# Input projection by seven block products, with K, Q, V, gate and x through DRAM, and attention after all projections

## The chip, the cores and the metric

One core of a Trainium2 chip runs the whole kernel. The metric is device time in microseconds. TensorE is called PE (its weight loads PEld), VectorE DVE, ScalarE ACT, GpSimd POOL, and SyncE SP; SP only issues transfers here.

## The reference

One decoder layer on 1024 tokens of width 1024, all in float32: a norm, one input projection, two kinds of heads side by side, an output projection, and a gated FFN.

```python
n = rmsnorm(h, mix_norm_w)
proj = n @ w_in                       # 1024 x 5648: [z 1024 | x 1024, B 256, C 256 | dt 16 | q 1024 | k 1024 | v 1024]
xbc = silu(causal_dwconv(xbc))        # width 4, along tokens
# SSD heads (16 of 64, 2 groups, state 128), in chunks of 128 tokens
cb = einsum("bclgn,bcsgn->bcgls", cm, bm)
y_diag = einsum("bcgls,bgecls,bcsgep->bclgep", cb, lmat, xdt)
y_off = einsum("bclgn,bcgepn,bgecl->bclgep", cm, prev_states, exp(a_cs))
y = (y_diag + y_off + x5 * d_skip) * silu(z), then a norm in each group, times ssd_norm_w
# differential attention (8 heads, two maps of 64, values of 128), causal, in blocks of 128 queries
p = softmax(where(mask, s, -inf)); w = p[0] - lam * p[1]; o = w @ v, then a norm in each head
h = h + concat(y_ssd, y_da) @ w_out
h = h + (silu(n2 @ w_gate) * (n2 @ w_up)) @ w_down
```

## The kernel before

**Precision.** A float32 factor is split into a high part in a short format (`hi`, a cast on ACT) and the rest (`lo`, a subtraction on DVE, both in `split`), and a product is three matmuls, hi x hi, hi x lo and lo x hi (`mm3`, lines 127 to 129). Transposes, the scan's products and the values' product (`o`) take float32 as it is; the trace shows two passes for each of the latter.

**Order.** The kernel is written as one sequence of tile operations. A scheduler then orders each engine's instructions, and may put later ones ahead where their inputs and buffers allow; only around the output projection's last part and the first FFN pair is PE's order kept as written. Pools of tiles set how far that goes: `big` (4 tiles of 16 KB for each partition, `B16`), `a4` (14 of 4 KB), `p4` (6), `cv` (4), `hx` (3), `raw` (2), `wh` and `wl` (3 each), and in PSUM `mm` (2 banks), `sc` (2 of two banks) and `ms` (2 banks).

**Stages.**
- The rows of x are normed (`norm_rows`), transposed and split (`norm_transpose`): `nhi` and `nlo`, two halves of 512 tokens, fill the four big tiles until the last head's Q.
- `proj_T` makes 128 columns of the projection as [columns, 512 tokens], 24 matmuls of 512 columns for each half of the tokens: for x, B and C (with the convolution), and for K and Q of each head. `proj_nat` makes 256 columns as [128 tokens, 256], for the gate and V; `proj_z0` the first gate columns together with the 16 of dt.
- The scan of a group of SSD heads (`ssd_scan`) runs over 8 chunks, each in three steps (`front`, `middle`, `back`); `back` stores the transposed y to `yT_d`. Its inputs `CT`, `Bn`, `CB` and `xn` stay in SBUF; the gate comes from `z_d` in DRAM.
- Attention runs over 8 heads and, in each, 8 blocks of 128 queries. A pair of heads gets its V by `v_pair`, a head its K and Q by `qk`, whose sinks write `KS`, `QH` and `QL` straight from PSUM. For each block and each of the two maps, PE makes scores `s` in one of the two `sc` buffers, DVE adds the mask and takes the maximum, ACT does the exponential and its sum, DVE combines the maps (line 596), PE transposes the weights (`wtp`), ACT copies them, and PE multiplies by V (`o`, line 611). `att_back` of a block comes after `att_front` of the next.
- The output projection takes `yT_d` back in four groups of 512 rows (`load_y`: weighted by the norm's weights as it is split), adding each group's 256-column products to the sums in DRAM or SBUF: `po_s` for the first group, `po_a` for the next two, `po_b` for the last.
- The FFN's gate and up projections, and then the down projection, are made by seven products of half-size blocks (Winograd's form) instead of eight: sums of weight blocks on POOL (`sub`), sums of the normed rows' blocks once ahead (`turn` and `room` make their transposed, split operands), and sums of the products by adding on in PSUM and reading between (`ORDER`).

Of the kernel before, what the change touches and what calls it, by code (L numbers as in the profile page):

```python
# [24 lines left out]
def tile_hybrid_block(  # L25
# [86 lines left out]

    def norm_transpose(parts, wbc, his, los, t, xn, pts, name, pool=()):
        norm_rows(parts, wbc, [xn], name, pool)
        tk = slice((t % 4) * P, (t % 4) * P + P)
        for q in range(2):
            pt = pts([P, 4, P], f"pt_{name}_{q}")
            for j in range(4):
                k = q * 4 + j
                nc.tensor.transpose(pt[:, j, :], xn[:, k * P:(k + 1) * P], ident)  # L120
            hi = his[t // 4][:, q * 4:q * 4 + 4, tk]
            lo = los[t // 4][:, q * 4:q * 4 + 4, tk]
            nc.scalar.copy(hi, pt)
            nc.vector.tensor_tensor(lo, pt, hi.bitcast(F32), op=ALU.subtract)
# [45 lines left out]
    def split(hi, lo, raw, scale=None):  # L170
        if scale is None:
            nc.scalar.copy(hi, raw)  # L172
            nc.vector.tensor_tensor(lo, raw, hi.bitcast(F32), op=ALU.subtract)  # L173
# [17 lines left out]
    def z0_unit(raw, a, u):
        hi = wp.tile([P, 4, 264], F32R, tag="wh", bufs=3, name=f"wh_z0_{a}_{u}")
        lo = wp.tile([P, 4, 264], F32R, tag="wl", bufs=3, name=f"wl_z0_{a}_{u}")
        split(hi, lo, raw)
        return hi, lo

# [49 lines left out]


    def proj_T(*jobs):
        """each job: a weight, a column, a name and sink(half, psum [128 columns, 512 tokens])"""
        us = [w_unit(w_k[:, :, col:col + P], [P, KD, P], name) for w_k, col, name, _ in jobs]  # L250
        for half in range(2):
            for (hi, lo), (_, _, name, sink) in zip(us, jobs):
                ps = MM([P, 512], f"mm_{name}_{half}")
                for k in range(KD):
                    mm3(ps, hi[:, k, :], lo[:, k, :], nhi[half][:, k, :], nlo[half][:, k, :], k == 0, k == KD - 1)
                sink(half, ps)

    def proj_z0(us, name, sink):
        """units of 264 columns; sink(t, psum [128 tokens, 264])"""
        for t in range(NT):  # L260
            ps = (MS if t % 4 > 1 else MM)([P, 264], f"mm_{name}_{t}")
            tk = slice((t % 4) * P, (t % 4) * P + P)
            for k in range(KD):
                hi, lo = us[k // 4]
                mm3(ps, nhi[t // 4][:, k, tk], nlo[t // 4][:, k, tk], hi[:, k % 4, :], lo[:, k % 4, :],
                    k == 0, k == KD - 1)
            sink(t, ps)

    def proj_nat(col, name, sink):
        """256 columns; sink(t, psum [128 tokens, 2 blocks from t, 256])"""  # L270
        us = [w_unit(w_in_k[:, 4 * u:4 * u + 4, col:col + 256], [P, 4, 256], f"{name}_{u}") for u in range(2)]
        for t in range(0, NT, 2):
            ps = MM([P, 2, 256], f"mm_{name}_{t}")
            for i in range(2):
                tk = slice(((t + i) % 4) * P, ((t + i) % 4) * P + P)
                for k in range(KD):
                    hi, lo = us[k // 4]
                    mm3(ps[:, i, :], nhi[t // 4][:, k, tk], nlo[t // 4][:, k, tk], hi[:, k % 4, :], lo[:, k % 4, :],
                        k == 0, k == KD - 1)
# [55 lines left out]
    def conv_tiles(*tiles):  # L335
        jobs = []
        for ct, name, acc in tiles:
            u_ = CV([P, T], F32, "u_" + name)
            jobs.append((ct, name, acc, u_))

        def wk(ct, k):
            return pcol[:, CW + k * 12 + ct:CW + k * 12 + ct + 1]

        def sink_of(ct, name, acc, u_):
            def sink(half, ps):
                sl = slice(half * 512, half * 512 + 512)
                nc.scalar.copy(u_[:, sl], ps)
                nc.scalar.activation(acc[:, sl], ps, AF.Identity, bias=pcol[:, CB + ct:CB + ct + 1], scale=wk(ct, 3))
            return sink
        proj_T(*[(w_in_k, C_X + j[0] * P, j[1], sink_of(*j)) for j in jobs])  # L350
        for ct, name, acc, u_ in jobs:
            for sh in (1, 2, 3):
                nc.vector.scalar_tensor_tensor(acc[:, sh:], u_[:, :T - sh], wk(ct, 3 - sh), acc[:, sh:],
                                               op0=ALU.mult, op1=ALU.add)
            nc.scalar.activation(acc, acc, AF.Silu)

    def gate_dt():
        """the gate of group 0 and dt"""
        for a in range(2):
            zt = [None]  # L360
            w0, w = (0, 248) if a == 0 else (248, 264)

            def sink(t, ps):
                if t % 2 == 0:
                    zt[0] = CV([P, 2, w], F32, f"zt0_{a}_{t}")
                if a == 0:
                    nc.vector.tensor_tensor(adt[:, t, :], ps[:, 0:16], hv[:, 0, :], op=ALU.add)
                nc.scalar.activation(zt[0][:, t % 2, :], ps[:, 264 - w:], AF.Silu)
                if t % 2 == 1:
                    nc.gpsimd.dma_start(z_d[t - 1:t + 1, :, w0:w0 + w].rearrange("t p c -> p t c"), zt[0])  # L370
            proj_z0(zus if a == 0 else [z0_unit(z0_raw(1, u), 1, u) for u in range(2)], f"z0_{a}", sink)

    def gate(g):
        for hf in range(2):
            zt = [None]
            zc = g * 512 + hf * 256

            def sink(t, ps):
                if t % 4 == 0:
                    zt[0] = CV([P, 4, 256], F32, f"zt{g}_{hf}_{t}")  # L380
                nc.scalar.activation(zt[0][:, t % 4:t % 4 + 2, :], ps, AF.Silu)
                if t % 4 == 2:
                    nc.gpsimd.dma_start(z_d[t - 2:t + 2, :, zc:zc + 256].rearrange("t p c -> p t c"), zt[0])
            proj_nat(C_Z + zc, f"z{g}_{hf}", sink)

    def ssd_inputs(g):
# [27 lines left out]
        for j in range(4):  # L414
            xc = CV([P, T], F32, f"xc{g}_{j}")
            conv_tiles((g * 4 + j, f"x{g}_{j}", xc))
            if prev is not None:
                turn(j - 1, prev)
# [663 lines left out]
```

## Time and profile before

| | |
|---|---|
| Median of three runs | 1643.02 us (1641.4 to 1645.18) |
| Profiled execution: its span, with nothing shown around it | 1643.3 us |
| Busy: PE, DVE, ACT, POOL | 1597.2, 1071.6, 775.8, 429.2 us |
| Projections, scans and attention, by the trace | start to about 840 us |
| Rest of the output projection, then FFN and final norm | 840 to 960, 960 to 1643 us |

How to read it: "PE busy" joins modelled matmul times, so a busy PE streams without a pause, though one matmul's time (0.39 us for 512 columns) overlaps the next's; the pace is the time between two starts. In a row of groups stand the line, the engine, the operation, out<-in by tile names, the shape and the count, then the sum of busy time, the mean of one in ns, and the engine's idle time just ahead of them with who ended it.

### The profile page before, as it was taken

The page shows a single profiled execution, that of the slowest core. Times are in us where ns is not written, and L with a number is a line of the kernel's source. Part 1 is how long each engine was busy: PE and PEld are TensorE (multiplying, and loading weights), DVE is VectorE, ACT ScalarE, POOL GpSimd, SP SyncE. Part 2 cuts the span into 40 slices and gives each one's busy share as a digit, 9 for nine tenths or more (in the row PEclk, how much of TensorE's full clock was granted, in tenths as well). Part 3 has the DMA queues.
Part 4 walks back from the last instruction along what each step waited for, and adds up shares of the span by engine and source line. Part 5 has one row for each costly group of instructions (what it writes and reads, how often), then busy time and mean ns, then how long its engine had stood idle before and what let it go on. Part 6 is the DMA issues. An engine that isn't in the chain of part 4 may idle for free. (4 is left out here: it accounts for less than half of the span.)

```text
span 1643.3 us, 23716 instructions
## 1 busy us (share of the span) xinstructions
PE 1597.2 (97%) x9170; PEld 1386.9 (84%) x9170; DVE 1071.6 (65%) x1682; ACT 775.8 (47%) x1608; POOL 429.2 (26%) x378
## 2 busy tenths in 40 slices
PE   6999999999999999999999998999999999999997
PEld 6988878887989989889999987888888888778885
DVE  5345745688776676677674477455555555898987
ACT  6444764456555565575552245333333333334445
POOL 4100330032000000013300034444444443542322
PEclk9999999999999999999999999999999999999999
DMA  5321451143011110147523221233333323944122
GB/s 195 110 79 52 129 163 56 36 142 92 24 46 39 46 33 27 45 130 229 162 77 116 84 99 56 96 102 104 111 116 118 98 96 134 365 166 186 39 103 103
DMA packets 105291, 172.78 MB, mean 105 GB/s; under 512 B 7813, under 2 KB 75530, under 8 KB 103770
## 3 DMA queue, kind: packets, MB, share of 16 engines
q1 hardware_dynamic: 95210, 137.11, 25.2%
q0 software_dynamic: 9968, 34.15, 6.3%
q8 instruction: 72, 1.18, 0.3%
q14 instruction: 41, 0.34, 0.1%
HBM read 125.82 MB, written 45.42 MB: 104 GB/s over the span
## 5 line engine op out<-in xcount | busy, mean ns | idle before, releaser
L127 PE MATMUL x<-n,wa 128*128 128x512 f32 x352 | 138.7, 396 | 0.0
L128 PE MATMUL x<-n,wa 128*128 128x512 f32 x352 | 138.7, 394 | 0.0
L129 PE MATMUL x<-n,wa 128*128 128x512 f32 x352 | 137.8, 394 | 0.0
L590 ACT ACTIVATE p<-s,nmx 128x256 f32<-128x256 f32 (+7 forms) x128 | 94.4, 740 | 53.2 <-DVE nmx L588 49.9
L172 ACT CAST wa<-s 128x512 fp32r<-128x512 f32 x88 | 54.7, 622 | 132.3 <-PE x L129 59.4
L173 DVE TENSOR_TENSOR wa<-s,wa 128x512 fp32r<-128x512 f32 x88 | 76.8, 873 | 51.1 <-ACT wa L172 50.8
L172 ACT CAST dg<-gd 128x512 fp32r<-128x512 f32 x77 | 47.7, 620 | 114.7 <-PE dx L129 57.2
L588 DVE TENSOR_REDUCE nmx<-s 128x1 f32<-128x256 f32 (+7 forms) x128 | 95.3, 754 | 2.4
L173 DVE TENSOR_TENSOR dg<-gd,dg 128x512 fp32r<-128x512 f32 x77 | 66.2, 862 | 23.3 <-ACT dg L172 23.2
L129 PEld LDWEIGHTS x<-n,wa 128*128 128x128 f32 x352 | 66.5, 189 | 15.1
L128 PEld LDWEIGHTS x<-n,wa 128*128 128x128 f32 x352 | 66.6, 189 | 14.8
L127 PEld LDWEIGHTS x<-n,wa 128*128 128x128 f32 x352 | 66.6, 189 | 14.8
L127 PE MATMUL mm_z<-wh_z,nhi 128*128 128x264 f32 (+1 forms) x256 | 75.9, 298 | 2.3 <-ACT wh_z L172 2.3
L611 PE MATMUL o<-v,p 128*128 128x128 f32 x576 | 77.7, 275 | 0.0
L129 PE MATMUL mm_z<-wh_z,nlo 128*128 128x264 f32 (+1 forms) x256 | 77.3, 303 | 0.0
L611 PEld LDWEIGHTS o<-v,p 128*128 128x128 f32 x576 | 73.5, 191 | 2.7
L128 PE MATMUL mm_z<-wl_z,nhi 128*128 128x264 f32 (+1 forms) x256 | 75.0, 294 | 0.0
L127 PE MATMUL mm_v<-wh_v,nhi 128*128 128x256 f32 x256 | 74.2, 290 | 0.0
L129 PE MATMUL mm_v<-wh_v,nlo 128*128 128x256 f32 x256 | 74.1, 290 | 0.0
L128 PE MATMUL mm_v<-wl_v,nhi 128*128 128x256 f32 x256 | 73.5, 287 | 0.0
L128 PE MATMUL po_a<-wl_wo,yh 128*128 128x256 f32 x256 | 72.6, 283 | 0.0
L91 POOL TENSOR_TENSOR rs_o<-ms_o,mhalf 128x4 f32<-128x4 f32 x16 | 18.0, 1125 | 208.4 <-DVE ms_o L89 208.3
(331 smaller groups left out, 5172.9 us busy)
## 6 DMA issues: line engine op xcount, KB each, us to landing
gd<-g_d SPq DMA_DIRECT2D x11, 1792.0 KB, 7.8
wr_g<-in_w_gate_dram SPq DMA_DIRECT2D x22, 512.0 KB, 3.8
wr_u<-in_w_up_dram SPq DMA_DIRECT2D x22, 512.0 KB, 4.3
g_d<-sg SPq DMA_DIRECT2D x22, 512.0 KB, 5.1
wr_d<-in_w_down_dram SPq DMA_DIRECT2D x22, 512.0 KB, 5.0
L<-cs_d POOLq DMA_DIRECT2D x16, 512.0 KB, 4.4
wr_y<-yT_d SPq DMA_DIRECT2D x16, 512.0 KB, 3.8
wr_wo<-in_w_out_dram SPq DMA_DIRECT2D x16, 512.0 KB, 3.5
```

Of the source, the lines that this page charges most:

```text
L91: nc.gpsimd.tensor_tensor(r, ms, mhalf[:, :w], op=ALU.pow)
L127: nc.tensor.matmul(ps, lh, rh, start=first, stop=False, skip_group_check=more)
L128: nc.tensor.matmul(ps, lh, rl, start=False, stop=False, skip_group_check=more)
L129: nc.tensor.matmul(ps, ll, rh, start=False, stop=last, skip_group_check=more)
L172: nc.scalar.copy(hi, raw)
L173: nc.vector.tensor_tensor(lo, raw, hi.bitcast(F32), op=ALU.subtract)
L588: nc.vector.reduce_max(nmx[:, m:m + 1], s[:, :Lk], axis=AX.X, negate=True)
L590: nc.scalar.activation(p[:, :Lk], s[:, :Lk], AF.Exp, bias=nmx[:, m:m + 1], accum_out=sm[:, m:m + 1])
L611: nc.tensor.matmul(o, wT[:, j * P:(j + 1) * P], vt[h % 2][j], start=(j == 0), stop=(j == i))
```

## The change

The input projection is made by the seven products too. The normed rows' seven operands (`room`, `turn`, now defined ahead) stand in the four big tiles (products 1, 2, 6, 5) and in twelve of the `a4` tiles (7, 3, 4) until the last projection. `in_pair` replaces `proj_T`, `proj_nat` and `proj_z0`: for two column tiles it makes seven products, the sums of weight blocks on POOL, and reads PSUM seven times, copying on ACT or adding on DVE. dt has matmuls of its own (`dt_cols`). What it yields goes to DRAM: `z_d`, `v_d`, `kT_d`, `qT_d`, `xn_d` (x transposed) and `bc_d` (C, B and their product), and is loaded again for each chunk or head; the scan and `qk` read from there.

The order written is: gate of group 0, dt, B, C, x; then the second gate and V with scan 0 woven in between products (`weave`), K and Q of head pairs with scan 1; then attention for all heads. The first two groups of the output projection are one (`po_s` over eight row tiles), `po_a` the third.

Other moves: the norms' weights are applied where y is stored (four ACT products for each chunk instead of a copy; `oT`), so `load_y` splits without a factor, with the subtraction on POOL; the subtractions for `KS` and `QL` are on POOL; the stores of `yT_d` and `h_d`, and the loads of x for the sums, are issued by SP instead of POOL.

```diff
+    def in_pair(a, s5, name, wide, outs, sink, scale=None):
+        sub(s5, a[1][0], a[1][1], ALU.add)
+        sub(a[1][0], a[0][0], a[1][0])
...
+        for p in ORDER:
...
+            src = {1: a[0][0], 2: a[0][1], 6: a[0][0], 5: s5, 7: a[1][0], 3: a[0][1], 4: a[1][1]}[p]
...
+            if wide:
+                for k0 in (0, 2):
+                    at = wp.tile([P, 2, 2, 256], F32R, tag="wh", bufs=3, name=f"wa_{name}_{p}_{k0}")
+                    split(at[:, 0], at[:, 1], src[:, k0:k0 + 2, :])
...
+            else:
+                at = wp.tile([P, 2, 4, P], F32R, tag="wh", bufs=3, name=f"wa_{name}_{p}")
+                split(at[:, 0], at[:, 1], src)
+                for k in range(4):
+                    mm3(ps[0], at[:, 0, k, :], at[:, 1, k, :], bh[k], bl[k], new and k == 0, k == 3, True)
...
-    gate_dt()
+    for _ in wide_pair(C_Z, "z0", sink_z(0), zraw, z0_out, P4([P, 4, 256], F32, "s5_z0")):
+        pass
+    dt_cols()
     decays()
-    ssd_scan(0, *ssd_inputs(0))
-    gate(1)
-    ssd_scan(1, *ssd_inputs(1))
+    for col, name, sk in ((C_B, "B", sink_bc("B")), (C_C, "C", sink_bc("C")), (C_X, "x0", sink_x(0)),
...
+    weave([(lambda: wide_pair(C_Z + 512, "z1", sink_z(1)), 14),
+           (lambda: wide_pair(C_V, "v0", sink_v(0)), 14),
+           (lambda: wide_pair(C_V + 512, "v1", sink_v(1)), 14)], ssd_scan(0), 30 / 42)
...
+           for h in range(0, NH, 2) for c, d, n, sc in ((C_K, kT_d, "k", None), (C_Q, qT_d, "q", 0.125))],
+          ssd_scan(1), 30 / 50)
...
     def qk(h):
...
+            kd, qd = [CV([P, 2, 512], F32, f"{n}d{h}_{half}") for n in "kq"]
+            for t_, src in ((kd, kT_d), (qd, qT_d)):
...
+            nc.scalar.copy(ks, kd)
+            for m in range(2):
+                b = slice(64 - 64 * m, 128 - 64 * m)
+                sub(ks[b, m, :], kd[b, m, :], ks[b, m, :].bitcast(F32))
+            split(qh, ql, qd, nc.gpsimd)
...
-            split(yh[:, j, :], yl[:, j, :], load_raw(yT_d[kt], [P, T], f"y{kt}"), scale=pcol[:, col:col + 1])
+            split(yh[:, j, :], yl[:, j, :], load_raw(yT_d[kt], [P, T], f"y{kt}"), nc.gpsimd)
...
-    ys = [load_y(0)]
+    ys = [load_y(0), load_y(1)]
...
-    for kg in (1, 2):
+    for kg in (2,):
```

Three places in the engines' orders. The first is PE at the first scores of head 0 (`s0_0_0`: head, block, map). Before, they stand among the products for K of head 1 (`mm_k1`), with the scan still going (`ytp1_6`):

```order
L127 MATMUL mm_k1_1_3785<-nhi1_135,wh_k1_3751 128x512
L585 MATMUL s0_0_0_3453<-KS0_0_3340,QH0_0_3406 128x128
L586 MATMUL s0_0_0_3453<-KS0_0_3340,QL0_0_3407 128x128
L128 MATMUL mm_k1_1_3785<-nlo1_137,wh_k1_3751 128x512
L129 MATMUL mm_k1_1_3785<-nhi1_135,wl_k1_3752 128x512
```

Now they stand behind the last product of the last Q (`x_q6`, product 4) and ahead of the output projection (`po_s`):

```order
L120 MATMUL x_q6_5118<-nn_4_3_156,wa_q6_4_5222 128x512
L121 MATMUL x_q6_5118<-nn_4_1_154,wa_q6_4_5222 128x512
L736 MATMUL s0_0_0_5287<-KS0_0_5263,QH0_0_5264 128x128
L736 MATMUL s0_0_1_5294<-KS0_0_5263,QH0_0_5264 128x128
L737 MATMUL s0_0_0_5287<-KS0_0_5263,QL0_0_5265 128x128
L737 MATMUL s0_0_1_5294<-KS0_0_5263,QL0_0_5265 128x128
L119 MATMUL po_s0_0_8217<-wh_wo0_0_8205,yh0_8167 128x256
```

The scores moved from amid projections to behind all of them.

The second is what feeds them now, first on SP (the stores of Q, `qT_d`; loads of y, `wr_y`; of head 0's K and Q, `kd0`, `qd0`):

```order
L159 DMA wr_y4_8187<-yT_d_63 128x1024
L639 DMA qT_d_73<-o_q6_1_5115 128x512
L709 DMA kd0_0_5257<-kT_d_72 64x2x512 x2
L159 DMA wr_y5_8191<-yT_d_63 128x1024
L639 DMA qT_d_73<-o_q6_0_5114 128x512
L639 DMA qT_d_73<-o_q6_1_5115 128x512
L159 DMA wr_y6_8195<-yT_d_63 128x1024
L709 DMA qd0_0_5258<-qT_d_73 64x2x512 x2
```

and on POOL (the subtractions for y, `yl0` and `yl1`, and for head 0):

```order
L164 TENSOR_TENSOR yl0_8168<-wr_y0_8169,yh0_8167 128x1024
L164 TENSOR_TENSOR yl0_8168<-wr_y1_8173,yh0_8167 128x1024
L164 TENSOR_TENSOR yl0_8168<-wr_y2_8177,yh0_8167 128x1024
L164 TENSOR_TENSOR yl0_8168<-wr_y3_8181,yh0_8167 128x1024
L164 TENSOR_TENSOR yl1_8186<-wr_y4_8187,yh1_8185 128x1024
L169 TENSOR_TENSOR KS0_0_5263<-kd0_0_5257,KS0_0_5263 64x512 x2
L164 TENSOR_TENSOR yl1_8186<-wr_y5_8191,yh1_8185 128x1024
L164 TENSOR_TENSOR yl1_8186<-wr_y6_8195,yh1_8185 128x1024
L164 TENSOR_TENSOR QL0_0_5265<-qd0_0_5258,QH0_0_5264 128x1024
```

Before, these operands came straight from PSUM; now the load of Q stands behind seven loads of y, and its subtraction behind seven of theirs.

The third is PE in head 5, block 6. Before, the output projection's first group fills the room between the scores:

```order
L585 MATMUL s5_6_0_6465<-KS5_1_6146,QH5_1_6217 128x384
L586 MATMUL s5_6_0_6465<-KS5_1_6146,QL5_1_6218 128x384
L607 MATMUL wtp5_4_0_6446<-ident_69,p5_4_0_6385 128x128 x4
L607 MATMUL wtp5_4_4_6452<-ident_69,p5_4_0_6385 128x128
L127 MATMUL po_s0_4_7847<-wh_wo0_0_7783,yh0_7763 128x256
L128 MATMUL po_s0_4_7847<-wl_wo0_0_7784,yh0_7763 128x256
```

Now attention's own work is all that stands there, from block 3 of head 5 to block 1 of head 6:

```order
L758 MATMUL wtp5_4_0_7288<-ident_74,p5_4_0_7227 128x128 x4
L736 MATMUL s5_6_0_7307<-KS5_0_7047,QH5_1_7062 128x512
L737 MATMUL s5_6_0_7307<-KS5_0_7047,QL5_1_7063 128x512
L736 MATMUL s5_6_0_7307<-KS5_1_7061,QH5_1_7062 128x384
L737 MATMUL s5_6_0_7307<-KS5_1_7061,QL5_1_7063 128x384
L758 MATMUL wtp5_4_4_7294<-ident_74,p5_4_0_7227 128x128
L762 MATMUL o5_4_7297<-v5_7039,p5_4_1_7236 128x128 x4
L736 MATMUL s5_6_1_7316<-KS5_0_7047,QH5_1_7062 128x512
```

In the new order, 27, 31 and 30 us worth of the first output products (at the pace of the rows of before) stand between the scores of heads 0, 1 and 2, 3 in head 3, and none behind.

More of the change, by code (lines that the diff above doesn't have):

```diff
@@ L191, in z0_unit, with split, sub @@
[L191 to L195, printed above, removed]
+    def split(hi, lo, raw, eng=nc.vector):
+        nc.scalar.copy(hi, raw)
+        eng.tensor_tensor(lo, raw, hi.bitcast(F32), op=ALU.subtract)
+    w_in_k = w_in2.rearrange("(k p) c -> p k c", p=P)
+    def sub(o, x0, x1, op=ALU.subtract, eng=nc.gpsimd):
+        eng.tensor_tensor(o, x0, x1, op=op)
+        return o
@@ new lines, in turn, with raw_wide @@
+    def turn(p, u, src, dst, bank, name="f"):
+        pt = bank([P, 4, P], f"pt_{name}{p}_{u}")
+        for k in range(4):
+            nc.tensor.transpose(pt[:, k, :], src[:, k * P:(k + 1) * P], ident)
+        for k in range(2):
+            hi, lo = [dst[e][k][:, :, u * P:u * P + P] for e in range(2)]
+            nc.scalar.copy(hi, pt[:, 2 * k:2 * k + 2, :])
+            nc.vector.tensor_tensor(lo, pt[:, 2 * k:2 * k + 2, :], hi.bitcast(F32), op=ALU.subtract)
+    def raw_wide(col, name):
+        a = [[None, None], [None, None]]
+        for i in range(2):
+            for j in range(2):
+                if i == 0:
+                    a[i][j] = wp.tile([P, 4, 256], F32, tag="raw", bufs=2, name=f"wr_{name}_{i}{j}")
+                else:
+                    a[i][j] = A4([P, 4, 256], F32, f"wr_{name}_{i}{j}")
+                yield nc.sync.dma_start(a[i][j], w_in_k[:, 4 * j:4 * j + 4, col + i * 256:col + i * 256 + 256])
+        yield a
@@ L245, in w_unit @@
         return hi, lo
[L248 to L267, printed above, removed]
@@ L357, in gate_dt @@
[L357 to L371, printed above, removed]
@@ L413, in ssd_inputs @@
-        prev = None
[L414 to L418, printed above, removed]
-            prev = xc
-        turn(3, prev)
-        return CT, Bn, CB, xn
+                nc.tensor.transpose(pt[:, j, :], src[:, (4 * q + j) * P:(4 * q + j + 1) * P], ident)
+            (nc.vector.tensor_copy if q else nc.scalar.copy)(ov[:, 4 * q:4 * q + 4, :], pt)
+        return ov
@@ new lines, in sink_bc, with sink @@
+    def sink_bc(which):
+        def sink(i, half, o):
+            if (i, half) not in ((0, 1), (1, 0)):
+                return
+            acc = bcs[which, i] = conv((8 if which == "B" else 10) + i, f"{which}{i}", o)
+            bview = bc_d[i].rearrange("t p w c -> p t w c")
+            if which == "B":
+                nc.sync.dma_start(bview[:, :, 1, :], turn_to(acc, o, f"btp{i}"))
+                return
+            nc.sync.dma_start(bview[:, :, 0, :], acc.rearrange("p (t c) -> p t c", c=P))
+            ov = o.rearrange("p (t c) -> p t c", c=P)
+            for q in range(2):
+                pt = MS([P, 4, P], f"cbp{i}_{q}")
+                for j in range(4):
+                    ck = slice((4 * q + j) * P, (4 * q + j + 1) * P)
+                    nc.tensor.matmul(pt[:, j, :], bcs["B", i][:, ck], acc[:, ck], start=True, stop=True)
+                nc.scalar.copy(ov[:, 4 * q:4 * q + 4, :], pt)
+            nc.sync.dma_start(bview[:, :, 2, :], ov)
+        return sink
```

448 lines of the change are left out of this document (265 added, 183 removed).

## The prediction

> **What bounds the kernel now.** I read the page's first part, then the table of stages, then the groups of instructions. The first two lines give the execution on which the sum is made: its span is 1643.3 us, with nothing around it that another row shows, and the median of the three timed runs (1643.02 us) is 0.3 us from it. About 0.2% (3.3 us) either way is what a measurement of this kernel can tell from no change.
>
> ```profile
> span 1643.3 us, 23716 instructions
> PE 1597.2 (97%) x9170; PEld 1386.9 (84%) x9170; DVE 1071.6 (65%) x1682; ACT 775.8 (47%) x1608; POOL 429.2 (26%) x378
> ```
>
> The stages, each row with its length, then busy time and count of PE, PEld, DVE, ACT and POOL:
>
> ```profile
> core 0: us, PE busy (x) PEld busy (x) DVE busy (x) ACT busy (x) POOL busy (x), PEclk, DMA share, GB/s
> 0.00:60.00 60.00, 44.91 (x326) 43.79 (x327) 32.13 (x58) 35.64 (x57) 20.26 (x24) 0.97 0.49 160
> 160.00:240.00 80.00, 75.89 (x518) 65.92 (x517) 56.75 (x85) 60.07 (x122) 29.92 (x33) 0.98 0.44 139
> 440.00:680.00 240.00, 240.00 (x1516) 215.42 (x1516) 161.15 (x315) 137.91 (x344) 13.00 (x16) 1.00 0.14 42
> 720.00:840.00 120.00, 115.49 (x920) 111.63 (x919) 91.90 (x177) 69.87 (x176) 34.24 (x46) 1.00 0.55 178
> 880.00:920.00 40.00, 40.00 (x340) 40.00 (x340) 20.03 (x23) 9.76 (x9) 0.00 (x0) 1.00 0.39 123
> 1080.00:1120.00 40.00, 40.00 (x175) 32.55 (x174) 20.55 (x26) 11.86 (x20) 17.43 (x12) 1.00 0.30 99
> ```
>
> PE is the bound nearly everywhere. In 440 to 680 us, inside attention, it never pauses, because head h's softmax lies under the K, Q and V products of the next heads: DVE is at 67%, ACT at 57%. The last two rows give paces: 1120 us begins after 175 matmuls of 512 columns in 40 us, 0.229 us each; the output projection's 256-column ones take 40/340 = 0.118 us. A 128x128 transpose or fp32 pass comes from this row and the L607 mean below: (1.03 - 0.27)/7 = 0.109 us.
>
> ```profile
> 105.45 1.03 PE L394 MATMUL btp<-ident,BT 128*128 128x128 f32 x8
> L607 PE MATMUL wtp<-ident,p 128*128 128x128 f32 x288 | 46.7, 273 | 1.2 <-ACT o L613 1.2
> L611 PE MATMUL o<-v,p 128*128 128x128 f32 x576 | 77.7, 275 | 0.0
> ```
>
> **What PE no longer does.** Seven of eight block products remain. Of 512 columns, x, B, C, K and Q had 1344 matmuls and have 1176: 168 x 0.229 = 38.5 us less. The gate and V had 1536 of 256 or 264 columns and have 1344 of 256: 192 x 0.118 + 1.4 us for the eight columns of dt = 24.1 us less. Added: dt by itself, 40 matmuls that stream 512 columns, 9.2 us, and eight small transposes, 0.9 us; 112 transposes of the normed rows instead of 64, 48 x 0.109 = 5.2 us. Net 47 us less PE work. The attention's, output projection's and FFN's own PE work is the same. If PE stayed as full as it is, the result would be 1596 us.
>
> **What loses its cover: attention.** K, Q and V are all finished first, so attention stands alone with the first half of the output projection (po_s, 768 x 0.118 = 91 us) as filler. The new order of PE spends that filler early: 27, 31 and 30 us of it stand between the scores of heads 0, 1 and 2, 3 us in head 3, none later; heads 4, 6 and 7 get some 23 us of po_a. Attention's own PE work in a head is 72 passes of o, 36 transposes, 48 score matmuls (24 of 512 columns, 8 each of 384, 256, 128) and 8 transposes of the output: 7.8 + 3.9 + 8.7 + 0.9 = 21.3 us. Heads 0 to 2 so hold 21.3 x 3 + 88 - 5 (the last blocks' o falls into the next head) = 147 us of PE work, heads 3 to 7 about 132 us.
>
> The other engines' share of a head:
>
> ```profile
> L590 ACT ACTIVATE p<-s,nmx 128x256 f32<-128x256 f32 (+7 forms) x128 | 94.4, 740 | 53.2 <-DVE nmx L588 49.9 <-PE s L586 2.6 <-ACT p L590 0.3
> L590 ACT ACTIVATION_READ_ACCUMULATOR p<-s,nmx 128x1 f32 x128 | 25.2, 197 | 0.0
> L608 ACT COPY p<-wtp 128x512 f32<-128x512 f32 (+2 forms) x96 | 45.2, 476 | 19.8 <-PE wtp L607 19.4
> L613 ACT ACTIVATE o<-o,r 128x128 f32<-128x128 f32 x64 | 23.3, 365 | 74.8 <-PE o L611 74.4
> L614 ACT ACTIVATE p<-o 128x128 f32<-128x128 f32 x64 | 20.2, 315 | 0.8
> L614 ACT ACTIVATION_READ_ACCUMULATOR p<-o 128x1 f32 x64 | 12.6, 196 | 0.0
> L625 ACT COPY oT<-otp 128x512 f32<-128x512 f32 x16 | 9.1, 571 | 5.5 <-PE otp L624 5.5
> L172 ACT CAST wh_q<-wr_q 128x1024 fp32r<-128x1024 f32 x8 | 8.4, 1053 | 0.4 <-PE mm_k L128 0.4
> 15.51 1.06 ACT L123 CAST nhi<-pt_n 128x512 fp32r<-128x512 f32 x2
> L588 DVE TENSOR_REDUCE nmx<-s 128x1 f32<-128x256 f32 (+7 forms) x128 | 95.3, 754 | 2.4
> L596 DVE SCALAR_TENSOR_TENSOR p<-p,rr,p 128x128 f32<-128x128 f32 (+3 forms) x64 | 52.3, 817 | 1.9
> L587 DVE TENSOR_TENSOR s<-s,cneg 128x128 f32<-128x128 f32 x128 | 36.8, 294 | 31.4 <-PE s L586 30.2
> L595 DVE TENSOR_SCALAR rr<-r,neglam,sm 128x1 f32<-128x1 f32 x64 | 17.4, 272 | 1.9
> L593 DVE RECIPROCAL r<-sm 128x2 f32<-128x2 f32 x64 | 10.5, 164 | 49.7 <-ACT p L590 49.3
> L618 DVE TENSOR_TENSOR o<-o,rs_o 128x512 f32<-128x512 f32 x16 | 11.0, 687 | 5.8 <-POOL rs_o L91 5.8
> ```
>
> ACT: the seven groups add up to 230.0 us, 28.8 a head; the four casts of K and Q loaded from DRAM (128x1024, 1.05 each) make it 33.0. That is the upper end. Two casts of some 0.585 us ended after 1.06, so neighbours overlap by 0.11; if all 70 did, a head would cost 25.3, the lower end. DVE: 223.3 us, 27.9 a head. So from head 3 on PE has 21 us of work in a head and ACT and DVE 25 to 33: PE waits for them.
>
> The Trainium skill's page "ScalarE: Activation LUTs" (section "What ACT_TABLE_LOAD costs") says that back-to-back ACTIVATEs overlap by about 93 ns. The cast row agrees at 110 ns; by the page's figure alone a head would cost ACT about 26.5 us.
>
> How far above that floor does a head run? I follow block 6 of head 5 in the new order. ACT does exp6_0 (1.2 with its accumulator read), o4 and its square (0.9), then waits for the transposes of block 5, which wait for DVE: reciprocal, rr, mask, p5 (1.0 for 768 columns), 0.2 + 0.3 + 0.3 + 1.0 = 1.8, and 0.9 for PE. Copy (0.6) ends at 3.3, exp6_1 at 4.4, copy and the cast of a later QH at 5.7, o5 at 6.2, oT at 6.8, and only then exp7_0. In those 6.8 us PE has 8 score matmuls, 7 + 4 transposes and 12 passes: 1.8 + 1.2 + 1.3 = 4.3 us. It is idle 37%, so a head takes 21.3/0.63 = 34 us. Heads 3 to 7: 5 x 34, plus nine casts of y and w_out (9.5), less eight of K and Q that heads 6 and 7 do not have (8.4): 171 us against 132. **Loss 39 us**; ends: 0 (ACT's lower end hides under PE) and 62 (a quarter more per head). Heads 0 to 2 hold more PE work (147 us) than ACT's 99 plus 8 for their own weights; at the 96% of row 720:840 they lose **6 us** (0 to 12). That row's own 4.5 us idle lies in this stage and falls away.
>
> **The change-over, a new wait.** In PE's new order the first scores of head 0 stand right behind the last product of q6, with nothing else ahead of po_s. They need QH and QL of head 0, hence a store of q6 (a slot of the pool is freed by it), a load, a cast, and a subtraction on POOL; POOL's order has seven subtractions of y (128x1024) ahead of it, and SP's queue has that load behind the y loads, whose two buffers POOL must free.
>
> ```profile
> wr_y<-yT_d SPq DMA_DIRECT2D x16, 512.0 KB, 3.8
> 19.55 2.40 POOL L108 TENSOR_TENSOR xm<-x,mixw 128x1024 f32<-128x1024 f32 x1
> 19.61 3.42 DVE L111 SCALAR_TENSOR_TENSOR xm<-x,rs_n,mixw 128x1024 f32<-128x1024 f32 x1 [0.77 <-POOL rs_n L91]
> 12.69 1.28 DVE L111 SCALAR_TENSOR_TENSOR xm<-x,rs_n,mixw 128x1024 f32<-128x1024 f32 x1 [0.38 <-POOL rs_n L91]
> ```
>
> With two buffers a y tile takes (3.8 + 1.05 + 2.4)/2 = 3.6 us. They can start when q6's first two products have freed their operands, five products or 60 x 0.229 = 13.7 us before PE runs dry: 7 x 3.6 + 2.4 - 13.7 = 14 us idle. If the loads are early, POOL alone decides: 8 x 2.4 - 13.7 = 5.5. I take **12** (5 to 20), nearer the first, since SP's queue puts the loads behind stores.
>
> **The projections themselves.** Each pair of tiles is now split seven times, its sums are made on POOL, and PSUM is read seven times:
>
> ```profile
> L173 DVE TENSOR_TENSOR wa<-s,wa 128x512 fp32r<-128x512 f32 x88 | 76.8, 873 | 51.1 <-ACT wa L172 50.8
> L1008 DVE TENSOR_TENSOR h<-dx,h 128x512 f32<-128x512 f32 x64 | 40.0, 679 | 1.5 <-PE dx L129 1.4
> L353 DVE SCALAR_TENSOR_TENSOR xc<-u_x,pcol,xc 128x1023 f32<-128x1023 f32 (+2 forms) x24 | 30.7, 1281 | 0.3
> L752 DVE TENSOR_TENSOR n<-pt_f,n 128x256 fp32r<-128x256 f32 x56 | 21.9, 417 | 2.5 <-ACT n L751 1.6
> L124 DVE TENSOR_TENSOR nlo<-pt_n,nhi 128x512 fp32r<-128x512 f32 x16 | 10.8, 687 | 12.9 <-ACT nhi L123 12.9
> L495 ACT COPY y<-ytp 128x512 f32<-128x512 f32 x16 | 9.3, 579 | 6.5 <-PE ytp L493 6.4
> L496 POOL DMA_DIRECT2D yT_d<-y x16 | 12.5, 779 | 26.6 <-ACT y L495 25.0 <-ACT L L445 1.6
> ```
>
> For x that is 7 x 0.87 + 3 x 0.68 + 6 x 1.28 + 1.4 = 17.2 us of DVE under 84 x 0.229 + 1.7 = 21 us of PE; for K and Q 8.1 and the scan's share under 19.2 and the scan's. The row 160:240 shows DVE at 71% and ACT at 75% of a scan with PE at 95%, and 1080:1120 the same seven-product pattern with PE full. So it stays under PE; I add **6 us** (0 to 20) for puts that stand behind the scan's exps. The start: PE was idle 15 us of the first 60, until the rows were normed, and still waits for them; DVE has 56 copies of 0.42 instead of 16 of 0.69 there, 12 us more beside 32 busy in 60, so they hide, or cost up to 6 of those 20. The weighting of y moves from the later split to the scan: four products of 0.365 instead of a copy of 0.58, 16 x 0.9 = 14 us of ACT, under PE. Stores move from POOL (0.78 us each to issue, which it saves) to SP's queue, with those of K, Q, V and x: DMA was at 14% in attention, so they hide, but a load behind them waits, as at the change-over. The rest is unchanged: cost nothing.
>
> **Sum.** 1643.3 - 47 + 39 + 6 - 4.5 + 12 + 6 = 1655 us.
>
> **Rivals.**
> (a) Attention runs near ACT's lower end, so that heads 3 to 7 take at most 31 us each (155): loss 23 instead of 39, the change-over 5, the heads before 3, projections 0. That gives 1643.3 - 47 + 23 + 3 - 4.5 + 5 = 1623 us, faster. For it: the overlap of ACT's neighbours. Against it: the chain through four engines with two score buffers. It decides the sign where heads, change-over and projections lose under 48 us together.
> (b) DVE and POOL collide. POOL now subtracts for K, Q and y, some 10 us a head, and a DVE operation on two SBUF tensors took 3.42 us beside a POOL one instead of 1.28. If half of the eight p<-p,rr,p a head meet one, at 2.1 us each, heads 3 to 7 gain 8 us each: 1643.3 - 47 + 79 + 6 - 4.5 + 12 + 6 = 1695 us.
> The Trainium skill's page "SBUF — State Buffer" (section "SBUF: two separate sides") says that DVE with two SBUF inputs and GpSimd take the shared port pair as an exclusive lock for a whole instruction. The pair of rows 3.42 and 2.40 agrees.
> (c) Projections fall behind: the reading of a bank between two products waits for ACT in its queue. At 5% of the 490 us of projections and scans, 25 instead of 6: 1674 us.
> (d) The saving does not come, since smaller products run at another pace: against it, the FFN's same products run at 0.229. Not given a chance of its own.
>
> **Chances.** My forecast (1640 to 1680) 0.47, (a) 0.28, (b) 0.10, (c) 0.15; a tenth of the whole falls within 0.2%, out of the forecast's low end. Faster 0.28, same 0.10, slower 0.62. Range 1622 to 1698, from (a) to (b); the forecast's own is 1638 to 1678.
>
> **What would show it.** After: PE at 95% or more until the last Q, then a gap of some 12 us; heads 0 to 2 nearly full; PE some 75% busy over heads 3 to 7, its waits on ACT's copies of p and on exps; the FFN unchanged. Wrong if heads 3 to 7 pass in 31 us or less each, or if PE falls under 93% in the projections.

## The result, and the profile after

The changed kernel took 1757.81 us (median of four runs, 1752.43 to 1761.64), the kernel before beside it 1643.81: a ratio of 1.0701 (95% interval 1.0676 to 1.0727). The forecast was 1655 us, its range ended at 1698. The profiled execution took 1752.43 us, its span is 1750.7. The page's head, of the changed kernel:

```profile
span 1750.7 us, 24111 instructions
...
PE 1602.4 (92%) x8906; PEld 1380.8 (79%) x8906; DVE 1144.3 (65%) x1735; ACT 826.5 (47%) x1759; POOL 635.4 (36%) x446
```

PE is busy 5 us longer than before, where 47 us less was forecast, and idle for 148 us instead of 46. The forecast's sum had 1550 us busy and 105 idle: the kernel is above it by 52 us of busy time and 44 of idle time. The stages, each row with its length, then the busy time of PE, PEld, DVE, ACT and POOL, the granted clock, and DMA:

```profile
0.00:60.00 60.00, 33.40 (x178) 29.70 (x179) 41.36 (x62) 32.37 (x66) 40.23 (x30) 0.86 0.39 130
...
105.00:154.00 49.00, 39.35 (x168) 31.38 (x168) 28.95 (x47) 18.99 (x31) 9.00 (x7) 0.86 0.16 48
154.00:240.00 86.00, 86.00 (x422) 72.35 (x421) 65.42 (x71) 48.39 (x71) 23.19 (x15) 1.00 0.44 129
240.00:411.00 171.00, 159.15 (x1201) 150.10 (x1200) 129.47 (x152) 95.60 (x213) 58.70 (x43) 0.96 0.50 158
411.00:598.00 187.00, 186.40 (x883) 151.14 (x881) 117.08 (x155) 87.58 (x200) 69.22 (x54) 1.00 0.48 150
598.00:613.00 15.00, 0.41 (x2) 0.44 (x2) 0.90 (x3) 5.83 (x7) 9.88 (x6) 0.61 0.88 262
613.00:786.00 173.00, 156.34 (x1195) 149.88 (x1195) 104.36 (x201) 94.44 (x228) 55.94 (x34) 0.95 0.53 150
786.00:994.00 208.00, 166.68 (x975) 143.34 (x974) 140.15 (x306) 134.56 (x362) 65.16 (x43) 0.85 0.31 92
...
1091.00:1750.70 659.70, 638.97 (x2831) 524.67 (x2829) 443.43 (x609) 254.39 (x460) 279.24 (x196) 1.00 0.35 126
```

Up to 598 us are the projections and scans, 598 to 613 the change-over, 613 to 786 heads 0 to 2, 786 to 994 heads 3 to 7 up to their last score, and from 1091 the FFN. Idle time is the length less PE's busy time. The column to look at is the clock, the granted share of TensorE's full rate: 0.86, 0.95 and 0.85 in stages where PE has long gaps, 1.00 where its gaps are few. In this trace the clock is only ever 1.00 or 0.50, so 0.85 over 208 us means 62 us at half rate. PE was busy in most of them, and what it did there took up to twice as long (one `o` matmul 569 ns, the median one 275). "Busy" hides that loss. As an estimate, I take it as half of the time in which a matmul ran at half clock: 26 us in heads 3 to 7 and 48 us in the whole span (before: 5).

| Place | forecast | measured | more than forecast |
|---|---|---|---|
| Projections and scans: idle and slow | 27 (21 of before, 6 new) | 65 (48.7 idle, some 17 by the clock) | 38 |
| Change-over | 12 | 14.6 | 3 |
| Heads 0 to 2 | 153 | 173 | 20 |
| Heads 3 to 7 | 171 | 208 | 37 |
| FFN | as before | 10 less | -10 |

These rows make 88 of the 97 us between 1655 and the profiled 1752; the rest was not followed up.

### The profile page after: what moved, and what is told of

Its sections match the earlier page's. It is cut to its first block, busy times and chain, and to the rows that moved or that the text cites. A ratio compares the mean times of both kernels' runs of the same rounds, so it can differ in the third digit from the quotient of the medians.

```text
span 1750.7 us, 24111 instructions
## 1 busy us (share of the span) xinstructions
PE 1602.4 (92%) x8906; PEld 1380.8 (79%) x8906; DVE 1144.3 (65%) x1735; ACT 826.5 (47%) x1759; POOL 635.4 (36%) x446
## 5 line engine op out<-in xcount | busy, mean ns | idle before, releaser
L736 PE MATMUL s<-KS,QH 128*128 128x512 f32 (+2 forms) x192 | 79.0, 413 | 39.8 <-ACT p L741 25.1
L762 PE MATMUL o<-v,p 128*128 128x128 f32 x576 | 90.6, 304 | 8.0 <-ACT p L759 7.6
L762 PEld LDWEIGHTS o<-v,p 128*128 128x128 f32 x576 | 82.0, 214 | 15.0 <-ACT p L759 13.8
L736 PEld LDWEIGHTS s<-KS,QH 128*128 128x128 f32 x192 | 41.1, 215 | 51.9 <-ACT p L741 32.3
L738 DVE TENSOR_TENSOR s<-s,cneg 128x128 f32<-128x128 f32 x128 | 37.4, 294 | 67.0 <-PE s L737 62.9
L120 PE MATMUL po_s<-wl_wo,yh 128*128 128x256 f32 x256 | 75.1, 294 | 4.0 <-DVE wl_wo L164 4.0
L119 PE MATMUL po_s<-wh_wo,yh 128*128 128x256 f32 x256 | 74.5, 293 | 4.0 <-ACT wh_wo L163 4.0
L121 PE MATMUL po_s<-wh_wo,yl 128*128 128x256 f32 x256 | 74.4, 291 | 0.0
L737 PE MATMUL s<-KS,QL 128*128 128x512 f32 (+2 forms) x192 | 70.7, 380 | 1.7 <-POOL QL L164 1.7
L120 PE MATMUL dx<-dw,dg 128*128 128x512 f32 x176 | 67.8, 392 | 3.2 <-DVE dw L164 3.2
```

The costliest lines, as they stand in the source:

```text
L119: nc.tensor.matmul(ps, lh, rh, start=first, stop=False, skip_group_check=more)
L120: nc.tensor.matmul(ps, lh, rl, start=False, stop=False, skip_group_check=more)
L121: nc.tensor.matmul(ps, ll, rh, start=False, stop=last, skip_group_check=more)
L736: nc.tensor.matmul(sc, QH[i // 4][:, m, qr], KS[c][:, m, :w], start=True, stop=False)
L737: nc.tensor.matmul(sc, QL[i // 4][:, m, qr], KS[c][:, m, :w], start=False, stop=True)
L738: nc.vector.tensor_tensor(s[:, qs], s[:, qs], cneg, op=ALU.add)
```

## Experiments

The kernel before ran beside each; its medians were 1641.5 to 1643.8 us. Ratios are to that kernel, with their 95% intervals; the changed kernel's is 1.0701 (1.0676 to 1.0727).

**e1: the output products spread by hand**

```diff
+    with tc.manual_schedule(engines={mybir.EngineType.PE}):
         for h in range(NH):
...
                 pm, r = att_front(h, i, *kq)
+                fill(0.5)        # some 8 products of the output projection
                 step(3)          # and as many between the transposes of p and o
```

> The first eight row tiles' output products (768 of 256 columns) are put by hand between the scores, the transposes and the values' products of heads 0 to 6, 16 or so per block of queries, where the changed kernel has all of them in heads 0 to 2; the third group (po_a) comes behind attention. Theory 'cover' (attention is slow because PE has nothing else to do in heads 3 to 7): attention from its first to its last score then holds 91 us of these products, 171 us of its own work and some 20 us of filling and draining, so it takes 300 to 330 us instead of 381, the po_a behind it 46 us, and the time is 1690 to 1715 us, with the granted clock at 1.00 nearly everywhere. Rival 'chain' (a head takes 43 us whatever PE has beside it, because ACT and DVE in turn set it): 8 x 43 + 46, some 1735 to 1760 us.

1767.35 us, 1.0773 (1.0747 to 1.0799): slower than the changed kernel, and neither theory's range holds it. Heads 1 to 5 took 46 to 47 us each, though PE had, by an estimate from the paces above, no more than 36 us of work in one. In this form "cover" brings nothing; but the run also fixes PE's order by hand, which e7 does not. Waits in heads 3 to 7 of e1 (who waited for whom: sum in us, times, longest):

```profile
DVE r L744 <- ACT p L741: 44.7, 29, 3.7
...
PE o L763 <- ACT p L759: 24.9, 21, 2.6
ACT p L741 <- DVE nmx L739: 24.5, 24, 2.8
...
ACT KS L713 <- DMA kd<-kT_d: 12.2, 5, 3.3
```

PE stands, in its written order, waiting before `o`, whose operand ACT has still to copy; ACT stands before loads of K.

**e2: more work for PE**

```diff
+        for again in range(2 if h >= 3 else 1):
             for j in range(i + 1):
                 nc.tensor.matmul(o, wT[:, j * P:(j + 1) * P], vt[j], ...
```

> In heads 3 to 7 the values' product o is made twice, the first pass thrown away: 360 passes, 39 us of useless PE work at full clock, nothing else changed. Theory 'clock' (in heads 3 to 7 PE's granted clock falls to half because it is busy less than half of a stretch of 3.4 us, and that costs 26 us there): with PE busier the clock stays nearer to 1.00, the 47 us of idle time take up the rest, and the time stays within 1745 to 1770 us, perhaps below the 1758 of the changed kernel. Rival 'work' (PE's own work lies on the path of each block): the 39 us are added, at half clock more, 1790 to 1830 us.

1764.79 us, 1.0744 (1.0726 to 1.0762): 7 us more for 39 us of useless work. Heads 3 to 7 of e2:

```profile
789.00:1010.00 221.00, 188.47 (x1315) 169.23 (x1314) 143.49 (x306) 136.79 (x367) 64.87 (x43) 0.95 0.28 86
```

The clock rose from 0.85 to 0.95 (24 us at half rate instead of 61), and the idle time fell from 41 to 33 us. The stage grew by 13 us, a third of the 39 that were put in; 9 went into idle time, and by the remaining 17 the rest of PE's work became shorter. That the clock is part of the loss is shown.

**e3: the decays later**

```diff
     dt_cols()
-    decays()
     for col, name, sk in ((C_B, "B", sink_bc("B")), ...
+        if name == "C":
+            decays()
```

> The decays (some 20 small DVE operations, then three products on PE) are written behind the pairs B and C instead of straight behind dt. Theory: in the changed kernel PE's queue waits there for DVE, 8 us idle and 4 us by the half clock behind it; this goes, and the time is 10 to 12 us less, 1746 to 1748 us. Rival: the first chunks of the scan, which need the decays by way of DRAM, then wait instead, and the time is the same, 1758.

1754.58 us, 1.0678 (1.0662 to 1.0694), 3 us less by the medians, with overlapping intervals, so no gain is shown for the whole kernel. The place itself, in the changed kernel (the wait) and in e3 (two stretches):

```profile
PE cps L440 <- DVE adt L437: 7.9, 1, 7.9
```

```profile
105.00:154.00 49.00, 46.13 (x219) 37.53 (x218) 38.03 (x53) 24.57 (x36) 11.66 (x8) 1.00 0.25 73
154.00:240.00 86.00, 82.49 (x396) 68.34 (x395) 61.15 (x68) 47.34 (x72) 23.14 (x14) 0.98 0.43 126
```

In the first stretch PE gained 6.8 us and the clock went from 0.86 to 1.00; in the second it lost 3.5 that it hadn't lost before. The last Q ended 3.5 us earlier, a third of what was expected.

**e4: y's low parts on DVE**

```diff
-            split(..., load_raw(yT_d[kt], [P, T], f"y{kt}"), nc.gpsimd)
+            split(..., load_raw(yT_d[kt], [P, T], f"y{kt}"))
```

> The low parts of y are subtracted on DVE again instead of POOL. Theory 'POOL's queue' (PE's 14.6 us at the change-over are the wait for POOL's seven subtractions of y): the gap falls to some 8 us, the time to 1748 to 1752 us. Rival 'SP's queue' (Q's load stands behind the stores of q6 and the loads of y, and ACT's casts behind those loads): the gap stays at 12 us or more, the time at 1755 to 1760.

1753.97 us, 1.0681 (1.0665 to 1.0697). PE's wait at the change-over, in the changed kernel and in e4:

```profile
PE s L736 <- POOL yl L164: 14.6, 1, 14.6
```

```profile
PE s L736 <- ACT QH L163: 14.0, 1, 14.0
```

The rival was right on the gap (the time lies between the two forecasts): with POOL out of the way the same wait stands on ACT's cast of Q. ACT in turn waited there for loads, more for those of y than for Q's (1.1 us) or K's (2.1):

```profile
ACT yh L163 <- DMA wr_y<-yT_d: 6.8, 4, 3.2
```

POOL was the last to come, not what set the time.

**e5 and e6: what the loads of K and Q cost**

```diff
# e5
-            nc.scalar.copy(ks, kd)
+            nc.gpsimd.tensor_copy(ks, kd)
-            split(qh, ql, qd, nc.gpsimd)
+            nc.gpsimd.tensor_copy(qh, qd)
+            sub(ql, qd, qh.bitcast(F32))
# e6
-        kq = qk(h)
+        kq = qk(h) if h < 3 else kq
```

> The casts of K and Q loaded from DRAM (KS and QH, four of 1.05 us a head) are made on POOL instead of ACT. Theory 'ACT's queue' (in heads 3 to 7 of the changed kernel ACT waited 20 us for the loads of K and Q with exps and copies queued behind, and the 20 casts there take 21 us): heads 3 to 7 fall from 41.6 to some 36 us each, and the time to 1725 to 1738 us. Rival 'chain' (from scores through maximum, exponential and combination to the next scores, whatever ACT does besides): 1750 to 1760. POOL then has 20 us of work a head; if K comes late by it, the time rises.

> Heads 3 to 7 use the K and Q of head 2: their loads, casts and subtractions are left out. It bounds what these cost together: by 'ACT's queue' heads 3 to 7 take 34 to 37 us each, the time is 1718 to 1738 us; by 'chain' they take 40 us or more, the time is 1748 to 1758.

e5: 1742.92 us, 1.0594 (1.0554 to 1.0633). e6: 1729.84 us, 1.0526 (1.0503 to 1.0549), 28 us less than the changed kernel. e6 leaves out the loads, casts and subtractions of K and Q in heads 3 to 7 and uses those of head 2 there, so it is a bound and not the same layer. e6's time is what the theory "ACT's queue" had forecast; e5's lies between the two theories. First what the changed kernel shows in heads 3 to 7 (the first two rows), then heads 3 to 7 of e5, then of e6, each with PE's wait for the score buffer:

```profile
PE s L736 <- ACT p L741: 21.7, 23, 2.3
...
ACT QH L163 <- DMA qd<-qT_d: 14.1, 6, 3.8
```

```profile
792.00:984.00 192.00, 150.63 (x948) 127.59 (x947) 151.04 (x307) 124.85 (x352) 83.30 (x57) 0.93 0.34 102
PE s L737 <- ACT p L742: 20.4, 21, 2.9
```

```profile
780.00:967.00 187.00, 152.85 (x995) 129.69 (x994) 138.48 (x309) 124.41 (x351) 28.09 (x19) 0.96 0.16 53
PE s L736 <- ACT p L741: 22.2, 25, 2.6
```

With the casts on another engine (e5) heads 3 to 7 are 16 us shorter, with no loads (e6) 21 us (the other 7 are gained in heads 0 to 2), and the clock comes back to 0.93 and 0.96 without any change to PE's work. The waits for the score buffer, added up, did not fall. What fell is the time at half clock:

| Heads 3 to 7, us | changed kernel | e5 | e6 |
|---|---|---|---|
| Length | 208 | 192 | 187 |
| PE idle | 41 | 41 | 34 |
| PE busy | 167 | 151 | 153 |
| Of the length, at half clock | 61, in 7 stretches | 27, in 5 | 14, in 2 |

So nearly all that e5 gains is PE's own work at a better clock. The trace of the changed kernel shows what the loads have to do with it: ACT starts the casts in its order, and one that waits for its load holds up the exponentials and copies behind it. At full clock ACT waited for 1.7 us or more for such a load six times in these heads (1.7 to 3.8 us), and each time a stretch at half clock began 1 to 5 us after the cast had started. The seventh stretch follows another wait (PE for DVE's combination of the maps, 3.9 us). ACT's own work in the stage fell by 10 us in both; the casts' time and the waiting for their loads are not separated further. "Chain" is not refuted, but what remains for it is 37 us a head, not 42, and part of that is still half clock. In e5 the change-over grew from 14.6 to 17.6 us; PE there waits for POOL's cast of head 0's Q.

**e7 and e8: the output products held back by buffers**

```diff
-        oT = P4([P, 512], F32, f"oT{h}_{q}")
+        oT = hx.tile([P, 512], F32, tag="hx", name=f"oT{h}_{q}")
...
+        for _ in range(8):       # one tile of 48 products, its sums in hx too
+            next(fills, None)
```

> The 768 output products are held back by buffers, 48 of them for each four blocks of queries, evenly over all eight heads; the order of the rest is left to the scheduler (in e1 it was written by hand); the third group comes behind attention. 'Cover': heads 0 to 2 fall from 58 to some 44 us each, heads 3 to 7 stay at 42 to 44 us, all eight 345 to 355 us instead of 381; with 16 us of po_a no longer inside, 1738 to 1750 us. By 'chain', and if 11 us of products a head still get in the way of attention's own, heads take 47 us as in e1, and the time is 1765.

> e5 and e7 together. If ACT's queue sets the length of a head, 8 heads at 38 to 40 us (PE has 33 us of work in each): 1700 to 1720 us. If the chain does: as e7.

e7: 1749.77 us, 1.0641 (1.0614 to 1.0668); from the first to the last score 359 us instead of 381 (345 to 355 were expected), the time at the upper end of what "cover" gave. e8: 1731.58 us, 1.0539 (1.0509 to 1.0568); 343 us. Both spread the same products as e1, with the order left to the scheduler, and e7 is 18 us faster than e1: a cover helps a little (8 us), and where its instructions stand counts for more than that. e8 missed its 1700 to 1720, since heads took 43 us, not 38 to 40, as a mean. Heads 3 to 7 of e8, with the products spread and the casts on POOL, run at nearly full clock:

```profile
757.00:958.00 201.00, 176.72 (x1280) 160.39 (x1281) 154.47 (x310) 121.75 (x349) 79.73 (x58) 0.99 0.39 115
```

**e9 and e10: the two ends, and all together**

```diff
-        sub(x0[:, J2], x0[:, J2], t2)
-        sub(x1[:, J1], x1[:, J2], x1[:, J1])
+        sub(x0[:, J2], x0[:, J2], t2, eng=nc.vector)
+        sub(x1[:, J1], x1[:, J2], x1[:, J1], eng=nc.vector)
...
-            kd, qd = [CV([P, 2, 512], F32, f"{n}d{h}_{half}") for n in "kq"]
+            kd, qd = [(CV if h else P4)([P, 2, 512], F32, f"{n}d{h}_{half}") for n in "kq"]
```

> Three edits of the changed kernel in stages far apart, each read from its own stage. (1) The two sums of rows per pair of row tiles, made on POOL at the start, go to DVE: by 'DVE and POOL in each other's way' (from 30 to 45 us DVE is busy 13.5 of 15 and POOL 15 of 15, one DVE subtraction of 512 columns takes 2.53 us, another 1.42) the last Q ends 5 to 8 us earlier than 598 us; if DVE is simply full there, no earlier or later. (2) The lambda sums, in the changed kernel just ahead of head 0 with ACT waiting 4 us for them, go behind the gate of group 0. (3) Head 0's K and Q are loaded into tiles of the pool p4, free since scan 1, instead of cv, where they wait for the last stores of Q, and its subtractions are made on DVE: by 'slots and queues' the 14.6 us of PE's wait for head 0's operands fall under 4, part of which then is the wait for the products of y. All three: 1735 to 1745 us. If the gap only moves to the first output products, 1750.

> Everything that helped: e3, e4, e5, e7 and the three edits of e9. The stages add up, if they don't share a cause: e8 at 1731.6, less 10 to 20 at the two ends, less 3 for the decays: 1700 to 1718 us. All of it leaves attention alone with the output projection; it isn't expected to reach the kernel before.

e9: 1742.11 us, 1.0617 (1.0594 to 1.064). The change-over is gone: head 0's first scores start 3 us before the last product of Q ends, and part of the gain is lost again: heads 0 to 2 take 171 us with 25 of them idle (173 and 17 in the changed kernel), although about 126 of their matmuls now fall later, and heads 3 to 7, which hold these, take 216 us instead of 208. The edits of that end (the lambda sums earlier, other slots for head 0's loads, its subtractions on DVE) were not tried one by one. The start gained nothing, the last Q ended at 598.3 us. One group of rows there, in the changed kernel and in e9:

```profile
L169 DVE TENSOR_TENSOR nt<-x,x 128x512 f32<-128x512 f32 x4 | 5.9, 1467 | 0.0
```

```profile
L169 DVE TENSOR_TENSOR nt<-x,x 128x512 f32<-128x512 f32 x4 | 2.7, 677 | 0.0
```

```profile
30.00:45.00 15.00, 8.69 (x48) 7.28 (x47) 15.00 (x17) 4.09 (x9) 8.82 (x4) 0.83 0.01 2
```

Beside POOL's sums a DVE sum took 1467 ns, without them 677. But with POOL's eight sums moved over, DVE is busy for 15.00 of 15 us (13.48 in the changed kernel), and PE is idle for as long in the first 60 us (26.8 and 26.6). The start is full on DVE.

e10: 1702.02 us, 1.0366 (1.0333 to 1.0399), near the low end of what was expected: the stages' gains add up, and nearly half of the 114 us is repaid. The rest was not divided; the last Q ends at 597 us (598 in the changed kernel), and attention still takes 335 us.

**e11 and e12: why the unchanged FFN ran faster**

```diff
# e12, on the kernel before
-        raw = wp.tile([P, 4, 264], F32, tag="raw", ...
+            raw = wp.tile([P, 4, 256], F32, tag="raw", ...      # dt and 240 columns
+            raw = wp.tile([P, k.stop - k.start, 272], F32, tag="raw", ...  # the other 272, three row blocks
```

> The kernel before, unchanged, profiled on the chip of these runs. In the first profile its FFN products of 512 columns start every 230 ns, in every profile of the changed kernel and its variants every 227, in the same code. If the program makes the difference, they start every 230 ns here too; if it was that one execution, every 227, and the profile's FFN takes some 9 us less.

> The kernel before, with one edit at its start: the gate's first columns and dt are made as 256 and 272 columns instead of twice 264, the second in units of three row blocks. With that the weight slots (raw, wh, wl) are 4096 bytes apart instead of 4224, and every large tile lies at the same remainder of its address by 512, as in the changed kernel. Nothing behind the first 75 us is changed otherwise. Theory 'placement' (where the weight tiles lie sets the pace of the 512-column products): the FFN's products start every 227 ns instead of 230, the FFN takes 651 us instead of 660, K, Q and x gain some 5 us more: 1626 to 1634 us. Rival (something else in the changed program, such as the instruction order or the queues): the pace stays at 230 ns, the time at 1640 to 1645.

e11 (the kernel before again, one run, 1638.39 us) and then e12, the FFN's first group of products:

```profile
L127 PE MATMUL x<-n,wa 128*128 128x512 f32 x352 | 139.1, 397 | 0.0
```

```profile
L127 PE MATMUL x<-n,wa 128*128 128x512 f32 x352 | 136.7, 390 | 0.0
```

The starts are 230 ns apart in e11 as in the first profile, and 227 in e12. e12 took 1629.13 us, 0.9918 (0.9906 to 0.9931): it is faster than both kernels. The weight slots of the kernel before are 4224 bytes, because of one stage with 264 columns at the very start, and the products of 512 columns behind it run 1.3% slower for it in the FFN (K, Q and x, at 232 to 233 ns instead of 227, some 2%). Whether the slots' distance or their remainder by 512 counts, and whether for the weights or the streamed operand, stays open.

## Why the prediction was wrong, point by point

**PE's work: the saving was right in size, but it is not what sets the end.** The seven products ran as forecast: 1176 matmuls of 512 columns for K, Q, x, B and C and 1344 of 256 for the gate and V, started every 227 and 120 ns. The busy time doesn't show it: -47 forecast, -11 from the FFN's faster products, some +43 by the half clock make -15, and +5 was measured. Of the 20 us between, 14 lie in the heads: without the clock's part they hold 152 us (0 to 2) and 141 us (3 to 7) of PE work, where 147 and 132 were forecast. Why was not followed up. The mean of an `o` matmul, 304 ns instead of 275, is no evidence for it: the median is 275 in both kernels, so the mean is raised by those at half clock.

**"A head takes 21.3/0.63 = 34 us": the step that failed.** It followed one block through the engines with PE's durations at full clock and with every operand of the head in place. 42 us a head were measured. For heads 3 to 7 the forecast was 132 us of PE work and 39 us of idle time; the trace has 41 us idle and 167 busy. So the idle time came out as forecast, in part by luck, since the late loads were not in it (e6, without them, has 34). What was wrong is the 132 us at full clock: some 26 of the missing 35 us are work done at half clock, 9 are more work than was priced. ACT's casts that wait for K and Q are ahead of six of the seven slow stretches, and without the loads a head takes 37 us (e6); more work for PE brings the clock back too (e2). I had put PE's idle share in a block at 37% myself and never asked what that does to the clock. The row 720:840 of before, from which I took "96%", shows 1.00; the row 0:60 with 0.97 I had quoted without asking why. By the signs that the prediction named, PE was 80% busy in heads 3 to 7 (75 forecast), half of its idle time there a wait for ACT's exponentials, as forecast; and it was 92% busy up to the last Q, under the 93% at which the prediction called itself wrong.

**"Heads 0 to 2 lose 6".** PE was 90% busy, not 96%, and the clock 0.95. Of the 173 us, 16 lie in the slow stretch that the change-over set off (4 us lost by the estimate above). The row of before from which the share came had no such start and no loads of K and Q; here ACT waited some 40 us for these, and PE 8 us for the split weights of the output projection.

**The change-over: 12 us forecast, 14.6 measured.** The wait stands where the forecast had put it, and POOL's y was the last to come. But POOL's queue was not the cause (e4); with the three edits of e9 the wait goes, and which of them does it is open.

**"Projections: 6 (0 to 20)".** From 411 to 598 us, seven products beside a scan, PE lost 0.6 us: that part of the forecast holds. What was missed lies earlier: 26.6 us idle in the first 60 instead of 15, and "so they hide, or cost up to 6" was wrong, since that DVE work is not spread over 60 us but stands between the rows and PE's first products (e9: 15.00 of 15 us); and the decays, costed at nothing, whose small DVE operations now stand behind PE's last dt transpose with PE's queue waiting 7.9 us (e3). Another 11.9 us are idle beside scan 0 (240 to 411 us), of which 6.5 are waits for the low parts of weights from DVE.

**Rival (b), DVE beside POOL:** not in attention. The combination of the maps took 882 ns instead of 817:

```profile
L747 DVE SCALAR_TENSOR_TENSOR p<-p,rr,p 128x128 f32<-128x128 f32 (+3 forms) x64 | 56.4, 882 | 1.6
```

That is 4 us in all heads, not 8 in each. At the start the sums on DVE took 1467 ns beside POOL's, 677 without (e9). **Rival (a)** (31 us a head) didn't come near. **Rival (c)**, 25 us lost in the projections, is nearer to the 44 measured than my 6, but not at its place: PE waited 0.2 us beside the scans for a bank that ACT had still to read. The prediction's sums come out; only the forecast's own span stands in it twice, as 1640 to 1680 us and as 1638 to 1678.

## What to carry to other kernels

Work that covers another stage's gaps can't be moved without pricing the gaps twice: once as idle time, and once as the slower clock that follows them. When operands go through DRAM, look at which in-order queue will stand waiting for the load, and what is queued behind it; put the cast on an engine that nobody waits for (e5), or load into buffers that come free early (part of e9). And a stage that needs an odd tile size can set the slots of a pool for the whole kernel.

## What the runs showed of the hardware that I had not expected

**In these traces the clock changes in steps of 3.41 us, and goes with the busy share of a step, not with one long pause.** Seven such steps in head 4 of the changed kernel (length, PE, PEld, DVE, ACT, POOL, clock, DMA):

```profile
836.95:840.36 3.41, 3.19 (x20) 2.21 (x18) 2.92 (x9) 2.89 (x13) 1.01 (x1) 1.00 0.42 114
840.36:843.78 3.42, 1.52 (x9) 0.73 (x7) 2.22 (x7) 1.67 (x5) 0.30 (x1) 1.00 0.19 43
843.78:847.19 3.41, 2.25 (x8) 2.06 (x9) 0.60 (x3) 2.16 (x6) 2.22 (x2) 0.50 0.21 77
847.19:850.60 3.41, 2.92 (x11) 2.35 (x10) 2.26 (x5) 1.54 (x5) 0.00 (x0) 0.50 0.74 216
850.60:854.01 3.41, 2.65 (x10) 2.05 (x9) 2.58 (x6) 3.09 (x5) 1.91 (x1) 0.50 0.71 250
854.01:857.43 3.42, 3.42 (x17) 3.32 (x16) 2.30 (x3) 2.69 (x6) 3.36 (x2) 0.50 0.40 118
857.43:860.84 3.41, 3.08 (x25) 2.85 (x24) 2.67 (x6) 2.85 (x8) 0.03 (x1) 1.00 0.69 194
```

In the second step PE is busy for 1.52 of 3.42 us, and the next runs at half clock; PE is then busy for 66 to 86% and stays slow; after a full step it is fast again. In this trace each of the 17 stretches at half clock follows a step in which PE was busy for 49% or less, and no step with over 50% was followed by one. The longest pause that touches the second step was 2.30 us, and part of it lies in the third. Another such step, in which no pause was longer than 0.66 us, and the one behind it:

```profile
871.07:874.48 3.41, 1.66 (x10) 1.05 (x10) 0.67 (x4) 3.38 (x9) 2.35 (x1) 1.00 0.21 77
874.48:877.89 3.41, 3.41 (x16) 3.41 (x17) 2.49 (x8) 1.60 (x6) 0.00 (x0) 0.50 0.55 154
```

The exact share isn't shown. In the changed kernel a step from 816.45 us, with PE busy for 1.67 of 3.42, kept the full clock, and in other traces fuller steps were followed by half clock, as here in e2 (2.13 of 3.41 us):

```profile
970.56:973.97 3.41, 2.13 (x14) 1.65 (x15) 0.03 (x1) 2.92 (x6) 0.00 (x0) 1.00 0.98 309
973.97:977.39 3.42, 3.42 (x19) 3.42 (x18) 2.99 (x8) 0.77 (x4) 0.00 (x0) 0.50 0.18 71
```

The Trainium skill's page "TensorE: Matmul & The Clock Gate" (section "HAM oscillation — how this bites in real kernels") gives as the rule "no PE-idle gaps >~3.4µs". By that, as an estimate, heads 3 to 7, with one pause over 3.4 us (3.92), would have slowed down about once; they did seven times. Where they differ, the measurement decides: shorter pauses, several of them within one step, are enough.

**The place of the weight tiles changes a 512-column product's pace by 1.3%:** 227 ns from start to start in e12, which changes the first stage alone and with it the size of the weight slots, and 230 in e11. The FFN, whose code is the same, took 661 us in e12 and 669 in e11.
